# Row-first delta blocks, early output weights, another bank order and a split last merge in a hybrid encoder layer

## The chip, the cores and the metric

The kernel runs on one core of a Trainium2 chip. A core has a matrix engine (TensorE, PE in the profile), three engines for elementwise work (VectorE or DVE, ScalarE or ACT, GpSimd or POOL) and SyncE (SP), which here issues most DMAs. Each engine works through its own list in order and waits on semaphores for others. The metric is device time in microseconds (us), the median of several runs.

## The reference

```python
def reference(x, mix_norm_gain, w_in, ..., w_ff1, w_ff2):     # SEQ = D_MODEL = 1024, D_FF = 4096
    u = rms_norm(h, mix_norm_gain)
    aq, ak, av, dqkv, dgate, da, db = jnp.split(u @ w_in, SPLITS, axis=-1)
    o_att = chunked_rel_attention(aq, ak, av, ...)      # 8 heads of 64, chunk 64 + 8 earlier chunks
    o_att = rms_norm(o_att, att_out_gain)
    dq, dk, dv = jnp.split(causal_short_conv(dqkv, dn_conv_w), 3, axis=-1)
    beta, log_decay = ...                               # from db and da
    o_dn = gated_delta_rule(dq, dk, dv, log_decay, beta)   # 4 heads of 128, triangular solve per chunk
    o_dn = rms_norm(o_dn, dn_out_gain) * jax.nn.silu(dgate)
    h = h + jnp.concatenate([o_att, o_dn], axis=-1) @ w_out
    z = rms_norm(h, ffn_norm_gain) @ w_ff1
    return h + jnp.square(jax.nn.relu(z)) @ w_ff2
```

One layer in float32: one projection for both mixers, band attention and a gated delta rule side by side, an output projection with the residual, and a feed-forward part of two large products.

## The kernel before

**Precision.** Every large float32 operand is split in two float32r parts, a high half (suffix `_h`, a cast on ACT) and a low half (`_l`, a subtraction on DVE or POOL); a product is three matmuls, high-high, high-low, low-high (`mm3`, L222). `split` (L203 and L204) records both halves, so these two lines stand for all operands, and the tile's name tells which.

**Stages.** Projections of delta q, k, v, gate, attention k and q run until about 290 us; `delta_prep` runs beside them. Attention and the chunked delta recurrence are interleaved until about 547, `out_proj` (tiles `op`, 4 groups of 96 matmuls) until 648, `ff1` (`q`, `yy`) until 954, `ff2` (`p`, `y`) to the end. `ff1` and `ff2` are seven-product schemes on 2 x 2 blocks.

**What sets the order.** The code is written as generators. In `attention` a planner (`Clock`, with costs per step) picks which generator goes on: score, turn, flip, a delta step, values, or a step of `outputs_gen`. The framework's scheduler then orders the instructions of each engine by priority (program order, raised inside `tc.high_priority()`) and by its own timeline; `tc.issue_after` holds an instruction behind another. Tiles come from pools with a fixed number of slots: a new tile waits until the last reader of the old one in its slot is done. The pool `wr` has 3 slots and holds raw weights (`wo_4_r` and so on), some attention pages (`t_pb`) and the residual pages `op_x`.

**Delta blocks.** `delta_prep` writes a 128 x 128 matrix per chunk and head to DRAM (`a_dr`), reads its 32 x 32 diagonal blocks back as 128 small systems (`ad`), inverts them by 31 steps on DVE, and writes the inverses (`x_dr`) and their transposes (`y_dr`). `delta_low(b)` (b = 0 in the projection stage, b = 1 in the attention stage) loads inverses and off-diagonal blocks into `l_xa` (L633, L634) and transposes into `l_w` (L630), then multiplies on PE in the 32 x 32 tiles `l_p` (L640, L649). `delta_merge` goes from 64 to 128. Later `c_` tiles are the recurrence: `c_kt`, `c_jv`, `c_jg`, `c_jq` are its loads, `c_att` the masked scores, `c_po` the output, `mixd` the gated result.

**Attention tiles.** `t_sa` and `t_sb` are scores, `t_pa` and `t_pb` probabilities, `t_tpa` and `t_tpb` their transposes on PE ("flips"), copied to `t_ta` and `t_tb`; `t_o` is the product with values, `t_on` its transposed and normalised form, `mixa` the result.

**Output projection.** `mixed` splits `mixd` and `mixa` into `mh` and `ml`; `weights(j)` loads eight 128 x 512 pieces of `w_out` in the order 4, 5, 6, 7, 0, 1, 2, 3 and splits them into `wo_k_h` and `wo_k_l`, the low halves by turns on POOL and DVE (`lo_turn`); `rows` does the matmuls and adds the residual (`h`, L1223).

**Banks.** The eight PSUM banks are dealt to pools in the order in which the pools are made: `ps_a` (3), `ps_t` (2), `ps_o` (1), `ps_d` (2). `op` lies in `ps_a`. After the mixer the same banks are dealt again to `psw` of `ff1` and `ff2`, in tiles of two banks.

**End.** In the last block of `ff2`, `merge` adds one accumulator to another in two halves of 128 x 1024; `store` issues two DMAs of the result. The last product is done by rows, and its four parts are subtracted (L1566) and stored one after the other.

Of the kernel before, what the change touches and what calls it, by code (L numbers as in the profile page):

```python
# [43 lines left out]
NV = 6  # L44
# [54 lines left out]
def hymba_kernel(  # L99
# [31 lines left out]
    mpool = mixer.enter_context(tc.tile_pool(name="mpool", bufs=1))  # L131
    ps_a = mixer.enter_context(tc.tile_pool(name="ps_a", bufs=3, space=PS))
    ps_t = mixer.enter_context(tc.tile_pool(name="ps_t", bufs=2, space=PS))
    ps_o = mixer.enter_context(tc.tile_pool(name="ps_o", bufs=1, space=PS))
    ps_d = mixer.enter_context(tc.tile_pool(name="ps_d", bufs=2, space=PS))

    def page(tag, name, dt=F32, w=512):
# [64 lines left out]
    def split(src, hi, lo, hi_eng, lo_eng):  # L202
        a = nc.scalar.copy(hi, src) if hi_eng is nc.scalar else hi_eng.tensor_copy(hi, src)  # L203
        return a.ins, lo_eng.tensor_tensor(lo, src, hi.bitcast(F32), ALU.subtract).ins  # L204

    lo_turn = [0]

    def load_w(src, name, tags=("wh", "wl")):
        raw = page("wr", name + "_r")
        nc.sync.dma_start(out=raw, in_=src)  # L210
        hi = page(tags[0], name + "_h", F32R)
        lo = page(tags[1], name + "_l", F32R)
        lo_turn[0] += 1
        split(raw, hi, lo, nc.scalar, nc.gpsimd if lo_turn[0] % 2 else nc.vector)
        return hi, lo
# [77 lines left out]
    dg_dr = dram.tile([NT, P, 4, P], F32, name="dg_dr")  # L293
    a_dr = dram.tile([NT, P, 512], F32, name="a_dr")
    x_dr = dram.tile([NT * 4, 32, 4, 32], F32, name="x_dr")
    y_dr = dram.tile([NT * 4, 32, 4, 32], F32, name="y_dr")
    kt_dr = dram.tile([NT, P, 512], F32, name="kt_dr")
# [248 lines left out]
    def delta_prep(kT, ab):  # L546
# [4 lines left out]
        for c in range(NT):  # L551
            n = f"d{c}"
            h4 = slice(4 * c, 4 * c + 4)
            tp = bank(ps_d, n + "_tp")
            four_t(tp, head(kT[c]))
            ss = sumsq(page("pp", n + "_sq"), "p", tp, n)
            if c + 1 < NT:
                kt = page("pp", n + "_kt")
                nc.vector.tensor_tensor(b4(kt), b4(tp), bc_row(ab["edec"][:, 1, h4]), ALU.mult)
                nc.sync.dma_start(out=kt_dr[c], in_=kt)  # L560
            yield 500
            L = decay("pp", n + "_L", ab, h4, tri_s, tri_ur, nc.vector)
            r = rsqrt("p", ss, 4, 1.0, EPS, n)
            br, br2 = ab["br"][:, h4], ab["br2"][:, h4]
            nc.gpsimd.tensor_tensor(br, ab["beta"][:, h4], r, ALU.mult)
            nc.gpsimd.tensor_tensor(br2, br, r, ALU.mult)
            nc.gpsimd.tensor_tensor(ab["nbr"][:, h4], br2, ab["ned"][:, h4], ALU.mult)
            yield 500
            mp = bank(ps_d, n + "_m")
            four(mp, lambda h, hs: kT[c][:, hs], lambda h, hs: kT[c][:, hs])  # L570
            A = page("pp", n + "_A")
            for h in range(4):
                hs = slice(h * P, (h + 1) * P)
                nc.vector.scalar_tensor_tensor(
                    A[:, hs], mp[:, hs], ab["br2"][:, 4 * c + h:4 * c + h + 1], L[:, hs],
                    ALU.mult, ALU.mult)
            nc.sync.dma_start(out=a_dr[c], in_=A)
            yield 900
# [3 lines left out]
        td = page("pp", "td")  # L582
        for c in range(NT):
            for b in range(4):
                bs = slice(32 * b, 32 * b + 32)
                p0 = 16 * c + 4 * b
                nc.sync.dma_start(out=ad[p0:p0 + 4],
                                  in_=a_dr[c].rearrange("r (h e) -> h r e", h=4)[:, bs, bs])
        nc.gpsimd.memset(xf, 0.0)
# [12 lines left out]
        for dst, src in ((x_dr, xd), (y_dr, ad)):  # L602
            for h in range(4):
                nc.sync.dma_start(out=dst[:, :, h, :], in_=src.rearrange("(q h) r e -> h q r e", h=4)[h])

# [11 lines left out]
    def delta_low(b, W, tag):  # L617
# [5 lines left out]
        Y = [w.rearrange("p (c h e) -> p c h e", c=2, h=4) for w in W[-2:]]  # L623
        a4 = a_dr[4 * b:4 * b + 4].rearrange("c r (h e) -> c r h e", h=4)
        for i in range(2):
            nc.gpsimd.memset(W[-2 + i], 0.0)
        for c in range(4):
            q = 16 * b + 4 * c
            for k in range(4):
                nc.sync.dma_start(out=Y[c // 2][32 * k:32 * k + 32, c % 2, :, 32 * (k % 2):32 * (k % 2) + 32],  # L630
                                  in_=y_dr[q + k])
            for r0 in (0, 64):
                nc.sync.dma_start(out=XA[r0:r0 + 32, c], in_=x_dr[q + r0 // 32])  # L633
                nc.sync.dma_start(out=XA[r0 + 32:r0 + 64, c], in_=a4[c, r0 + 32:r0 + 64, :, r0:r0 + 32])  # L634
        yield clock.now + 8000, "d"
# [22 lines left out]
    def delta_merge(c, W, res):  # L658
# [5 lines left out]
        Yd = W[c // 2].rearrange("p (c h e) -> p c h e", c=2, h=4)[:, c % 2]  # L664
        nc.sync.dma_start(out=A[64:128], in_=a_dr[c].rearrange("r (h e) -> r h e", h=4)[64:128, :, 0:64])
        nc.gpsimd.memset(Y[64:128, :, 0:64], 0.0)
# [161 lines left out]

    def attention(after, delta, values, outputs):

# [266 lines left out]
        while True:  # L1097
# [69 lines left out]
            elif k == "score":  # L1167
                g, t, pp = units[begun]
                score(g, t, pp)
                begun += 1  # L1170
                if pp and begun + 2 < len(units):
                    start(*units[begun + 2][0:2])
# [12 lines left out]

    def out_proj(result):


        order = (4, 5, 6, 7, 0, 1, 2, 3)
        w, parts, R, begun = [], [], {}, []  # L1190

        def weights(j):
            w.append([None] * NKT)
            for k in order:
                w[j][k] = load_w(w_out[k * P:(k + 1) * P, j * 512:(j + 1) * 512], f"wo{j}_{k}",
                                 (("wh", "u"), ("u", "wl"))[j])

# [37 lines left out]

        weights(0)
        mixed(0)
        acc = yield from rows(0, 0, None)
        weights(1)
        acc = yield from rows(1, 0, acc)  # L1240
# [174 lines left out]
    def ff2(psw, pools):  # L1415
# [52 lines left out]
        for kb in range(nb):  # L1468
# [70 lines left out]
            accumulate(1, product(f"p1{kb}", lambda i: (a11[i], b11[i])))  # L1539
            accumulate(5, product(f"p5{kb}", prep5))  # L1540
            accumulate(2, product(f"p2{kb}", lambda i: (a12[i], b21[i])))
# [13 lines left out]
            if last:  # L1555
                merge(nc.vector, 7, 6)
                merge(nc.vector, 4, 7)
                merge(nc.gpsimd, 5, 7)
                store(y[5], 1, 1, nc.scalar)
# [44 lines left out]
    ab = ab_proj(u)  # L1604
    W, result = [], {}
    after = []
# [5 lines left out]
    clock.reset()  # L1612
    rest = attention(after[NV - 1], delta_all(ab, kT, W), values, lambda: out_proj(result))
    for _ in rest or ():
# [52 lines left out]
```

## Time and profile before

| | |
|---|---|
| median of 3 runs | 1276.42 us (1275.62 to 1279.3) |
| profiled execution | 1273.11 us, span 1271.0 us |
| granted clock of TensorE, mean | 0.995 |
| PE busy | 1241.2 us, 98% of the span |
| DVE, ACT, POOL busy | 926.5, 547.6, 289.8 us |
| DMA | 158.53 MB, mean 125 GB/s |

The span counts from the first to the last recorded instruction; the execution's own time has 2.1 us around it. A matmul of 128 x 512 is shown with the time from its start to its end, which overlaps the next one's. The clock column is the share of full speed that the chip granted TensorE. "[3.63 <-issue]" behind an instruction says that its engine sat idle for 3.63 us before it and what ended that.

### The profile page before, as it was taken

How to read it: one execution, taken by the hardware profiler on the slowest of the kernel's cores; microseconds unless marked ns; L12 is line 12 of the kernel's file. 1: busy time of each engine (PE TensorE's matmuls, PEld its weight loads, DVE VectorE, ACT ScalarE, POOL GpSimd, SP SyncE). 2: the span in 40 equal slices, each digit the busy share in tenths (PEclk: the TensorE clock that was granted, in tenths of full speed). 3: DMA queues.
4: the chain of work that ended last, by engine and by line, in shares of the span. 5: the costliest groups of instructions: out<-in, count | busy, mean ns of one | idle time of the engine just before them, and what ended most of it. 6: DMA issues, size and time to landing. Idle time of an engine off the chain costs nothing.

```text
span 1271.0 us, 18018 instructions
## 1 busy us (share of the span) xinstructions
PE 1241.2 (98%) x6686; PEld 1033.3 (81%) x6686; DVE 926.5 (73%) x1388; ACT 547.6 (43%) x899; POOL 289.8 (23%) x487
## 2 busy tenths in 40 slices
PE   9999999999998999889999999999999999999998
PEld 8778878778888898778878788888887888888886
DVE  7899987654236577774349777677669997997988
ACT  7323132232245665654445454544445543333331
POOL 4425461344132345543210000000000000000034
PEclk9999999999999999989999999999999999999999
DMA  7214353564585532134441333332259623332002
GB/s 226 67 42 139 101 157 107 121 162 118 175 245 150 162 109 71 40 109 133 141 141 67 116 133 117 132 100 96 86 199 368 211 83 112 121 100 94 7 34 99
DMA packets 135398, 158.53 MB, mean 125 GB/s; under 512 B 31760, under 2 KB 79376, under 8 KB 134800
## 3 DMA queue, kind: packets, MB, share of 16 engines
q1 hardware_dynamic: 117216, 135.11, 35.0%
q10 hardware_dynamic: 18096, 22.29, 5.2%
q8 instruction: 52, 0.85, 0.3%
q14 instruction: 34, 0.28, 0.1%
HBM read 109.91 MB, written 47.45 MB: 124 GB/s over the span
## 4 chain that ended last, share of the span: by engine, by line
PE 51%; DVE 8%; issue 2%; ACT 1%; POOLq 1%; POOL 0%; DVEq 0%; ACTq 0%
PE p L1439 21%; PE q L1343 20%; PE op L222 6%; PE t_o L1024 1%; POOLq L1662 1%; DVE ml L204 1%; DVE h L1285 1%; DVE y L1511 0%; PE t_sa L925 0%; DVE q_0a_l L204 0%; DVE y L1507 0%; PE t_tpb L985 0%; DVE p43b_l L204 0%; DVE p73b_l L204 0%; DVE p43a_l L204 0%
## 5 line engine op out<-in xcount | busy, mean ns | idle before, releaser
L1511 POOL TENSOR_TENSOR y<-y,y 128x1024 f32<-128x1024 f32 x6 | 19.3, 3242 | 590.5 <-DVE y L1507 571.6
L1507 DVE TENSOR_TENSOR y<-y,p 128x1024 f32<-128x1024 f32 x46 | 55.1, 1216 | 5.4 <-PE p L1439 4.5
L222 PE MATMUL op<-mh,wo_l 128*128 128x512 f32 x128 | 50.1, 399 | 1.1 <-POOL wo_l L204 1.1
L222 PE MATMUL op<-mh,wo_h 128*128 128x512 f32 x128 | 50.6, 398 | 0.1
L222 PE MATMUL op<-ml,wo_h 128*128 128x512 f32 x128 | 50.2, 395 | 0.0
L945 DVE CUSTOM_DVE_ANT_0 t_pb<-t_sb,biasn 128x256 f32<-128x256 f32 (+1 forms) x64 | 23.2, 401 | 29.8 <-PE t_sb L925 29.8
L964 ACT ACTIVATE t_pb<-t_pb,t_nm 128x256 f32<-128x256 f32 (+1 forms) x64 | 31.4, 491 | 18.1 <-DVE t_nm L956 16.7
L1223 DVE TENSOR_TENSOR h<-op,op_x 128x512 f32<-128x512 f32 x16 | 10.8, 687 | 28.8 <-PE op L222 28.8
L1230 POOL TENSOR_TENSOR op_q<-op_q 128x512 f32<-128x512 f32 x14 | 19.6, 1397 | 47.3 <-ACT op_q L1229 47.2
L222 PEld LDWEIGHTS op<-mh,wo_l 128*128 128x128 f32 x128 | 24.4, 191 | 6.9 <-POOL wo_l L204 1.5
L222 PEld LDWEIGHTS op<-mh,wo_h 128*128 128x128 f32 x128 | 24.4, 191 | 5.9 <-issue 0.5
L222 PEld LDWEIGHTS op<-ml,wo_h 128*128 128x128 f32 x128 | 24.4, 190 | 5.2
L956 DVE CUSTOM_DVE_ANT_0 t_pa<-t_sa,biaso,t_nm 128x384 f32<-128x384 f32 (+2 forms) x48 | 25.0, 543 | 2.3 <-PE t_sa L925 2.0
L222 PE MATMUL g_ps<-uh,wg_h 128*128 128x512 f32 x64 | 25.3, 396 | 1.2 <-ACT wg_h L203 1.2
L968 ACT ACTIVATE t_pa<-t_pa,t_nm 128x384 f32<-128x384 f32 (+2 forms) x48 | 26.4, 550 | 0.0
L222 PE MATMUL aq_ps<-waq_h,uh 128*128 128x512 f32 x64 | 25.4, 400 | 0.8 <-ACT waq_h L203 0.8
L925 PE MATMUL t_sb<-ks,t_q 128*128 128x256 f32 (+1 forms) x144 | 24.0, 294 | 1.7 <-DVE t_nm L945 1.3
L222 PE MATMUL g_ps<-uh,wg_l 128*128 128x512 f32 x64 | 25.2, 393 | 0.4 <-POOL wg_l L204 0.4
L222 PE MATMUL dq_ps<-uh,wdq_h 128*128 128x512 f32 x64 | 25.5, 398 | 0.0
L222 PE MATMUL dv_ps<-uh,wdv_l 128*128 128x512 f32 x64 | 25.4, 397 | 0.0
L222 PE MATMUL dq_ps<-ul,wdq_h 128*128 128x512 f32 x64 | 25.3, 395 | 0.0
L222 PE MATMUL av_ps<-wav_l,uh 128*128 128x512 f32 x64 | 25.2, 394 | 0.0
(1109 smaller groups left out, 4306.7 us busy)
## 6 DMA issues: line engine op xcount, KB each, us to landing
wa<-in_w_ff_dram SPq DMA_DIRECT2D x32, 512.0 KB
a<-in_w_ff_dram SPq DMA_DIRECT2D x32, 512.0 KB
b<-f_dr SPq DMA_DIRECT2D x32, 512.0 KB
f_dr<-yy ACTq DMA_DIRECT2D x16, 512.0 KB
t_q<-q_dr SPq DMA_DIRECT2D x30, 256.0 KB
f_dr<-zz ACTq DMA_DIRECT2D x13, 512.0 KB
ks<-k_dr SPq DMA_DIRECT2D x16, 256.0 KB
wo_r<-in_w_out_dram SPq DMA_DIRECT2D x16, 256.0 KB
```

The lines of the kernel that those rows point to most:

```text
L204: return a.ins, lo_eng.tensor_tensor(lo, src, hi.bitcast(F32), ALU.subtract).ins
L222: nc.tensor.matmul(ps, a, b, start=(first and i == 0), stop=(last and i == n - 1))
L925: nc.tensor.matmul(o, q[m][:, i * P:(i + 1) * P], k[:, c], start=(m == 0), stop=(m == 1))
L945: nc.vector.tensor_tensor_reduce(sb[:, c], bk[:, c], new[g][pp][:, c], -1.0, 3.0e38, ALU.add, ALU.min, nm[:, 4 + i:5 + i])
L956: nc.vector.tensor_tensor_reduce(sa[e][:, 0:wa], bk[:, 0:wa], old[g][i][:, 384 - wa:384], -1.0, nm[:, 4 + i:5 + i], ALU.add, ALU.min, nm[: ...
L964: nc.scalar.activation(sb[:, c], sb[:, c], AF.Exp, bias=m, scale=-1.0, accum_out=T["sums"][:, 4 + i:5 + i])
L968: nc.scalar.activation(sa[e][:, 0:wa], sa[e][:, 0:wa], AF.Exp, bias=m, scale=-1.0, accum_out=T["sums"][:, i:i + 1])
L1230: nc.gpsimd.tensor_tensor(acc, acc, sq, ALU.add)
L1343: nc.tensor.matmul(part(ps, q), l[:, s], r, start=(k + m == 0), stop=(k == 3 and m == 2))
L1439: nc.tensor.matmul(part(ps[q], 0) if by_rows else part(ps[q // 2], q % 2), l[:, s], part(r, k), start=(i + k + m == 0), stop=(i + k + m == 4))
L1507: nc.vector.tensor_tensor(y[i][m], y[i][m], ps[m], op)
L1511: eng.tensor_tensor(y[i][m], y[i][m], y[z][m], ALU.add)
```

## The change

Six edits. (1) `a_dr`, `x_dr` and `y_dr` lie in DRAM with the row within a block first and the block second, so that several chunks go in one DMA: the loads of `ad` become 16 instead of 32, of each `delta_low` 4 instead of 16 for `l_xa` and 8 instead of 16 for `l_w`; the 128 systems of `ad` are ordered accordingly. (2) The first half of the output weights is emitted inside `attention`, right behind the last score, at high priority, instead of at the start of `out_proj`. (3) All low halves of output weights are made on DVE. (4) The pool `ps_a` is made last of the four bank pools. (5) The second product (`p5`) of `ff2`'s first block is emitted at high priority. (6) The second half of the last addition of `y[7]` to `y[5]` is done on DVE instead of POOL.

```diff
-    ps_a = mixer.enter_context(tc.tile_pool(name="ps_a", bufs=3, space=PS))
     ps_t = mixer.enter_context(tc.tile_pool(name="ps_t", bufs=2, space=PS))
     ps_o = mixer.enter_context(tc.tile_pool(name="ps_o", bufs=1, space=PS))
     ps_d = mixer.enter_context(tc.tile_pool(name="ps_d", bufs=2, space=PS))
+    ps_a = mixer.enter_context(tc.tile_pool(name="ps_a", bufs=3, space=PS))
...
-    def load_w(src, name, tags=("wh", "wl")):
+    def load_w(src, name, tags=("wh", "wl"), low=None):
...
-        split(raw, hi, lo, nc.scalar, nc.gpsimd if lo_turn[0] % 2 else nc.vector)
+        split(raw, hi, lo, nc.scalar, low or (nc.gpsimd if lo_turn[0] % 2 else nc.vector))
...
-    a_dr = dram.tile([NT, P, 512], F32, name="a_dr")
-    x_dr = dram.tile([NT * 4, 32, 4, 32], F32, name="x_dr")
-    y_dr = dram.tile([NT * 4, 32, 4, 32], F32, name="y_dr")
+    a_dr = dram.tile([P, NT, 512], F32, name="a_dr")
+    x_dr = dram.tile([32, NT * 4, 4, 32], F32, name="x_dr")
+    y_dr = dram.tile([32, NT * 4, 4, 32], F32, name="y_dr")
...
-        for c in range(NT):
+        for c in range(0, NT, 2):
             for b in range(4):
                 bs = slice(32 * b, 32 * b + 32)
-                p0 = 16 * c + 4 * b
-                nc.sync.dma_start(out=ad[p0:p0 + 4],
-                                  in_=a_dr[c].rearrange("r (h e) -> h r e", h=4)[:, bs, bs])
+                p0 = 4 * (NT * b + c)
+                nc.sync.dma_start(out=ad[p0:p0 + 8],
+                                  in_=a_dr[:, c:c + 2].rearrange("r c (h e) -> (c h) r e", h=4)[:, bs, bs])
...
-            for h in range(4):
-                nc.sync.dma_start(out=dst[:, :, h, :], in_=src.rearrange("(q h) r e -> h q r e", h=4)[h])
+            for p0 in range(0, P, 32):
+                nc.sync.dma_start(out=dst.rearrange("r q h e -> (q h) r e")[p0:p0 + 32], in_=src[p0:p0 + 32])
...
-        for c in range(4):
-            q = 16 * b + 4 * c
+        for r in range(2):
+            q = 2 * r * NT + 4 * b
+            nc.sync.dma_start(out=XA[64 * r:64 * r + 32], in_=x_dr[:, q:q + 4])
+            nc.sync.dma_start(out=XA[64 * r + 32:64 * r + 64],
+                              in_=a4[64 * r + 32:64 * r + 64, :, :, 64 * r:64 * r + 32])
+        for i in range(2):
             for k in range(4):
-                nc.sync.dma_start(out=Y[c // 2][32 * k:32 * k + 32, c % 2, :, 32 * (k % 2):32 * (k % 2) + 32],
-                                  in_=y_dr[q + k])
-            for r0 in (0, 64):
-                nc.sync.dma_start(out=XA[r0:r0 + 32, c], in_=x_dr[q + r0 // 32])
-                nc.sync.dma_start(out=XA[r0 + 32:r0 + 64, c], in_=a4[c, r0 + 32:r0 + 64, :, r0:r0 + 32])
+                q = k * NT + 4 * b + 2 * i
+                nc.sync.dma_start(out=Y[i][32 * k:32 * k + 32, :, :, 32 * (k % 2):32 * (k % 2) + 32],
+                                  in_=y_dr[:, q:q + 2])
...
                 begun += 1
+                if begun == len(units):
+                    with tc.high_priority():
+                        weights()
...
+    def out_weights(w, j):
+        w.append([None] * NKT)
+        for k in order:
+            w[j][k] = load_w(w_out[k * P:(k + 1) * P, j * 512:(j + 1) * 512], f"wo{j}_{k}",
+                             (("wh", "u"), ("u", "wl"))[j], nc.vector)
...
-        weights(0)
         mixed(0)
         acc = yield from rows(0, 0, None)
-        weights(1)
+        out_weights(w, 1)
...
-            accumulate(5, product(f"p5{kb}", prep5))
+            with tc.high_priority() if not kb else ExitStack():
+                ps = product(f"p5{kb}", prep5)
+            accumulate(5, ps)
...
-                merge(nc.gpsimd, 5, 7)
+                for m, eng in enumerate((nc.gpsimd, nc.vector)):
+                    eng.tensor_tensor(y[5][m], y[5][m], y[7][m], ALU.add)
                 store(y[5], 1, 1, nc.scalar)
...
-    rest = attention(after[NV - 1], delta_all(ab, kT, W), values, lambda: out_proj(result))
+    rest = attention(after[NV - 1], delta_all(ab, kT, W), values,
+                     lambda: out_weights(w_o, 0), lambda: out_proj(result, w_o))
```

**SP at the loads of delta block 1** (`l_xa<-x_dr`: inverses, `l_xa<-a_dr`: off-diagonal blocks, `ks`, `t_q`: attention loads). Before:

```order
L633 DMA l_xa<-x_dr 32x128
L634 DMA l_xa<-a_dr 32x4x32
L858 DMA ks_3991<-k_dr 128x512
L858 DMA ks_3993<-k_dr 128x512
L633 DMA l_xa<-x_dr 32x128
L703 DMA c_kt<-kt_dr 128x512
L634 DMA l_xa<-a_dr 32x4x32
```

Twelve more `l_xa` loads follow, again by turns from `x_dr` and `a_dr`, and then `c_jv`. Now:

```order
L907 DMA t_q<-q_dr 64x2x512 x2
L629 DMA l_xa<-x_dr 32x512
L630 DMA l_xa<-a_dr 32x16x32
L860 DMA ks_3955<-k_dr 128x512
L860 DMA ks_3957<-k_dr 128x512
L629 DMA l_xa<-x_dr 32x512
L705 DMA c_kt<-kt_dr 128x512
L630 DMA l_xa<-a_dr 32x16x32
L702 DMA c_jv<-dv_dr 128x512
```

Four loads are left, each with four chunks, and the last one stands behind `c_kt`, where the fourth stood.

**PE at the end of attention** (`mh`, `ml`: the mixers' result, high and low; `wo_4`: the first piece of the output weights). Before:

```order
L1001 MATMUL t_tpa_6515<-ident,t_pa_6327 128x128 x3
L516 MATMUL c_po<-c_vn,c_att 128x128 x4
L222 MATMUL op_6685<-mh_6650,wo_4_h 128x512
L222 MATMUL op_6742<-mh_6650,wo_4_h 128x512
L222 MATMUL op_6785<-mh_6650,wo_4_h 128x512
L222 MATMUL op_6685<-ml_6651,wo_4_h 128x512
L222 MATMUL op_6742<-ml_6651,wo_4_h 128x512
L222 MATMUL op_6785<-ml_6651,wo_4_h 128x512
L1001 MATMUL t_tpa_6521<-ident,t_pa_6334 128x128 x3
L985 MATMUL t_tpb_6533<-ident,t_pb_6403 128x128 x4
L1001 MATMUL t_tpa_6540<-ident,t_pa_6415 128x128 x3
L1001 MATMUL t_tpa_6546<-ident,t_pa_6422 128x128 x3
```

Now:

```order
L1051 MATMUL t_on<-ident,t_pb_6116 128x128 x2
L1003 MATMUL t_tpa_6507<-ident,t_pa_6271 128x128 x3
L222 MATMUL op_6629<-mh_6594,wo_4_h 128x512
L222 MATMUL op_6686<-mh_6594,wo_4_h 128x512
L222 MATMUL op_6729<-mh_6594,wo_4_h 128x512
L516 MATMUL c_po<-c_vn,c_att 128x128 x4
L222 MATMUL op_6629<-ml_6595,wo_4_h 128x512
L222 MATMUL op_6629<-mh_6594,wo_4_l 128x512
L222 MATMUL op_6629<-mh_6598,wo_5_h 128x512
L222 MATMUL op_6686<-ml_6595,wo_4_h 128x512
L222 MATMUL op_6686<-mh_6594,wo_4_l 128x512
L222 MATMUL op_6686<-mh_6598,wo_5_h 128x512
```

The 36 matmuls of pieces 4 to 7 for three rows of `op` stand ahead of the second `t_tpb` flip; before, only six did.

**DVE at the same place.** Before, from the last read of a row's maximum on:

```order
L956 ISA t_nm 128x1
L807 SCALAR_TENSOR_TENSOR mixd_6009<-c_tpo,dng,c_jg 128x4x128
L780 TENSOR_TENSOR c_att<-c_mt,c_Lt 128x512
L1051 TENSOR_TENSOR t_on<-t_on,t_tot 128x256
L204 TENSOR_TENSOR ml_6651<-mixd_4680,mh_6650 128x512
L786 TENSOR_TENSOR c_o<-c_o,c_po 128x512
L204 TENSOR_TENSOR ml_6655<-mixd_4680,mh_6654 128x512
```

And further down, the first low halves of the output weights that DVE made:

```order
L1036 RECIPROCAL t_tot<-t_tot 128x4
L1006 COPY t_ta_6550<-t_tpa_6546 128x384
L204 TENSOR_TENSOR wo_5_l<-wo_5_r,wo_5_h 128x512
L1068 TENSOR_TENSOR mixa_6257<-t_tpo,again 128x4x128
L204 TENSOR_TENSOR wo_7_l<-wo_7_r,wo_7_h 128x512
```

Now:

```order
L958 ISA t_nm 128x1
L204 TENSOR_TENSOR wo_4_l<-wo_4_r,wo_4_h 128x512
L204 TENSOR_TENSOR wo_5_l<-wo_5_r,wo_5_h 128x512
L204 TENSOR_TENSOR wo_6_l<-wo_6_r,wo_6_h 128x512
L809 SCALAR_TENSOR_TENSOR mixd_5953<-c_tpo,dng,c_jg 128x4x128
L782 TENSOR_TENSOR c_att<-c_mt,c_Lt 128x512
L1053 TENSOR_TENSOR t_on<-t_on,t_tot 128x256
L204 TENSOR_TENSOR ml_6595<-mixd_4624,mh_6594 128x512
L204 TENSOR_TENSOR ml_6599<-mixd_4624,mh_6598 128x512
```

The three low halves stand ahead of `mixd`, `c_att` and `t_on`.

**ACT behind it.** Now:

```order
L203 CAST mh_6602<-mixd_4624 128x512
L1058 ACTIVATE t_on,t_oss<-t_on 128x512
L203 CAST wo_7_h<-wo_7_r 128x512
L203 CAST mh_6606<-mixd_4624 128x512
L203 CAST wo_0_h<-wo_0_r 128x512
L203 CAST wo_1_h<-wo_1_r 128x512
L541 ACTIVATE c_po<-c_o 128x512
L203 CAST wo_2_h<-wo_2_r 128x512
L203 CAST wo_3_h<-wo_3_r 128x512
L1008 COPY t_ta_6511<-t_tpa_6507 128x384
L1008 COPY t_ta_6517<-t_tpa_6513 128x384
```

Before, no cast of a weight stood ahead of these copies: the rows from `t_on` on were

```order
L1056 ACTIVATE t_on,t_oss<-t_on 128x512
L203 CAST mh_6662<-mixd_4680 128x512
L541 ACTIVATE c_po<-c_o 128x512
L1006 COPY t_ta_6525<-t_tpa_6521 128x384
L203 CAST mh_6674<-mixa_5563 128x512
L203 CAST mh_6678<-mixa_5563 128x512
L991 COPY t_tb_6538<-t_tpb_6533 128x512
L1006 COPY t_ta_6544<-t_tpa_6540 128x384
L203 CAST wo_7_h<-wo_7_r 128x512
```

The two `t_ta` copies now stand behind five casts of weights (`wo_7_h` to `wo_3_h`).

Around `p50b_l` the rows of PE, DVE and ACT are the same as before.

More of the change, by code (lines that the diff above doesn't have):

```diff
@@ L576, in delta_prep @@
                     ALU.mult, ALU.mult)
-            nc.sync.dma_start(out=a_dr[c], in_=A)
+            nc.sync.dma_start(out=a_dr[:, c], in_=A)
             yield 900
@@ L623, in delta_low @@
         Y = [w.rearrange("p (c h e) -> p c h e", c=2, h=4) for w in W[-2:]]
-        a4 = a_dr[4 * b:4 * b + 4].rearrange("c r (h e) -> c r h e", h=4)
+        a4 = a_dr[:, 4 * b:4 * b + 4].rearrange("r c (h e) -> r c h e", h=4)
         for i in range(2):
             nc.gpsimd.memset(W[-2 + i], 0.0)
-        for c in range(4):
-            q = 16 * b + 4 * c
-            for k in range(4):
-                nc.sync.dma_start(out=Y[c // 2][32 * k:32 * k + 32, c % 2, :, 32 * (k % 2):32 * (k % 2) + 32],
-                                  in_=y_dr[q + k])
-            for r0 in (0, 64):
-                nc.sync.dma_start(out=XA[r0:r0 + 32, c], in_=x_dr[q + r0 // 32])
-                nc.sync.dma_start(out=XA[r0 + 32:r0 + 64, c], in_=a4[c, r0 + 32:r0 + 64, :, r0:r0 + 32])
+        for r in range(2):
[4 more added lines that the diff above has]
+        for i in range(2):
+            for k in range(4):
+                q = k * NT + 4 * b + 2 * i
+                nc.sync.dma_start(out=Y[i][32 * k:32 * k + 32, :, :, 32 * (k % 2):32 * (k % 2) + 32],
+                                  in_=y_dr[:, q:q + 2])
         yield clock.now + 8000, "d"
@@ L664, in delta_merge @@
         Yd = W[c // 2].rearrange("p (c h e) -> p c h e", c=2, h=4)[:, c % 2]
-        nc.sync.dma_start(out=A[64:128], in_=a_dr[c].rearrange("r (h e) -> r h e", h=4)[64:128, :, 0:64])
+        nc.sync.dma_start(out=A[64:128], in_=a_dr[:, c].rearrange("r (h e) -> r h e", h=4)[64:128, :, 0:64])
         nc.gpsimd.memset(Y[64:128, :, 0:64], 0.0)
@@ L827, in delta_all, with attention @@
             yield gens
-    def attention(after, delta, values, outputs):
+    def attention(after, delta, values, weights, outputs):
         def bias_page(tag, name):
@@ L1184, in attention, with out_proj @@
         return outputs_gen or outputs()
[L1186 to L1196, printed above, removed]
+    order = (4, 5, 6, 7, 0, 1, 2, 3)
+    def out_weights(w, j):
[3 more added lines that the diff above has]
+                             (("wh", "u"), ("u", "wl"))[j], nc.vector)
+    def out_proj(result, w):
+        parts, R, begun = [], {}, []
         def mixed(hf):
@@ L1604, in hymba_kernel @@
     ab = ab_proj(u)
-    W, result = [], {}
+    W, w_o, result = [], [], {}
     after = []
```

## The prediction

> **What bounds the kernel now.** I read the page's busy table first, then the list of what TensorE (PE) waited for, then stretches of time, then single engines.
>
> ```profile
> span 1271.0 us, 18018 instructions
> PE 1241.2 (98%) x6686; PEld 1033.3 (81%) x6686; DVE 926.5 (73%) x1388; ACT 547.6 (43%) x899; POOL 289.8 (23%) x487
> ```
>
> PE is busy for 98% of the span. The change removes no matmul, so all it can win is time in which PE waits or runs at a lowered clock, and the end behind the last matmul.
>
> ```profile
> PE l_p L640 <- issue: 3.6, 1, 3.6
> PE p L1439 <- DVE p50b_l L204: 1.8, 1, 1.8
> PE op L222 <- POOL wo_l L204: 1.1, 1, 1.1
> PE q L1343 <- DVE h L1223: 0.9, 1, 0.9
> PE aq_ps L222 <- ACT waq_h L203: 0.8, 1, 0.8
> 400.00:410.00 10.00, 6.37 (x87) 5.99 (x85) 3.99 (x14) 2.45 (x8) 2.30 (x8) 0.83 0.51 119
> 545.00:560.00 15.00, 11.11 (x60) 8.30 (x60) 10.97 (x20) 9.22 (x21) 8.89 (x16) 0.77 0.37 121
> 960.00:980.00 20.00, 18.21 (x81) 14.76 (x80) 18.53 (x17) 11.83 (x12) 0.00 (x0) 1.00 1.03 391
> ```
>
> The first five are waits (total, times, longest); every part of the change points at one of them. The last three are stretches: length, busy time of PE, of its weight loads, DVE, ACT, POOL, then granted clock. At 400 PE was idle 3.63 us and the clock was 0.83, which costs another 0.17 x 10 = 1.7. At 545 it was idle 3.89, and the clock of 0.77 cost 0.23 x 15 = 3.45. At 960 a wait of 1.79 left the clock at 1.00. So two places hold 5.3 and 7.3 us, and the others nothing but their waits.
>
> **Delta block 1, loads in fewer pieces.**
>
> ```profile
> DMA  4978699999999999999995121011021021021165
> 390.87 0.58 SPq L633 DMA_DIRECT2D l_xa<-x_dr  x1
> 403.56 0.55 SPq L634 DMA_DIRECT2D l_xa<-a_dr  x1
> 399.86 1.06 PE L516 MATMUL c_pq<-state,c_jq 128*128 128x128 f32 x8
> 404.55 1.44 PE L640 MATMUL l_p<-l_w,l_xa 32*32 32x32 f32 x32 [3.63 <-issue]
> ```
>
> These two SP rows are the first and last of 16 l_xa loads on SP's queue, one about every 0.6 us; PE begins l_p 0.44 us behind the last one's issue (404.11). So the wait that the profile calls "issue" is SP working through the list. Now four loads do it, each four times as large. The fifth to sixteenth (12 x 0.6 = 7 us or more) go, and the last stands where the third and fourth now stand, near 395.5; beside the transfers queued there it should land by 399, before 400.92, where PE is done with c_pq. PE's own order here is the same before and after. The wait and the clock loss go together: between 3.6 (clock dips anyway) and 5.3. I take 5.0, nearer the upper end, because the low clock starts right behind this wait. Late next would be t_q or c_jv, which move up on SP with it. New on SP: wo_4_r to wo_6_r stand earlier, between the l_w loads, and may wait there for a buffer that PE's t_on still reads. Behind them wait t_q and l_xa, but 16 fewer l_w issues (some 9 us) stand against it. I cost that at 0.
>
> The DMA line (the 40 slices of 388 to 406) shows the 16 DMA engines full until about 398 and nearly idle from there to 404. [...]
>
> **Delta block 0, in the projection stage.**
>
> ```profile
> 247.75 5.07 SPq L630 DMA_DIRECT2D l_w<-y_dr  x8
> 261.96 1.19 PE L640 MATMUL l_p<-l_w,l_xa 32*32 32x32 f32 x32
> 271.11 0.73 PE L222 MATMUL aq_ps<-waq_h,uh 128*128 128x512 f32 x2 [0.84 <-ACT waq_h L203]
> ```
>
> Here 8 x_dr loads become 2 and 16 l_w loads 8: 6 x 0.58 + 8 x 0.63 = 8.5 us less on SP, so the data that allowed l_p at 261.96 is there by 253.4. But the new order also puts l_p 39 rows earlier on PE, 39 x 0.23 (the pace of such rows, below) = 9 us, at 253.0. PE arrives as the data does: a wait of 0 to 1.5 (the 0.4 between them, and two loads more). Behind these loads the waq_r loads move up too, and the 0.84 wait for waq_h should go. Net between -0.84 and +1.5; I take -0.3, nearer to the wait that a row shows.
>
> **Output weights early, low halves on DVE.**
>
> ```profile
> 646.30 0.39 PE L222 MATMUL op<-mh,wo_h 128*128 128x512 f32 x1
> ...
> 647.45 0.39 PE L222 MATMUL op<-mh,wo_l 128*128 128x512 f32 x1
> 560.00:648.00 88.00, 87.70 (x411) 71.46 (x407) 33.62 (x41) 34.08 (x55) 27.54 (x26) 1.00 0.37 122
> 545.35 0.49 PE L1001 MATMUL t_tpa<-ident,t_pa 128*128 128x128 f32 x3
> 549.74 0.66 PE L985 MATMUL t_tpb<-ident,t_pb 128*128 128x128 f32 x4 [0.78 <-ACT t_on L1056]
> 555.56 0.80 PE L222 MATMUL op<-mh,wo_l 128*128 128x512 f32 x1 [1.14 <-POOL wo_l L204]
> 558.29 0.63 PE L222 MATMUL op<-mh,wo_l 128*128 128x512 f32 x1
> 553.92 3.28 POOL L204 TENSOR_TENSOR wo_l<-wo_r,wo_h 128x512 fp32r<-128x512 f32 x2
> 544.44 0.75 DVE L807 SCALAR_TENSOR_TENSOR mixd<-c_tpo,dng,c_jg 128x512 f32<-128x512 f32 x1
> 545.34 0.69 DVE L780 TENSOR_TENSOR c_att<-c_mt,c_Lt 128x512 f32<-128x512 f32 x1
> 555.54 6.13 SPq L210 DMA_DIRECT2D wo_r<-in_w_out_dram  x5
> 546.00 1.13 ACT L203 CAST mh<-mixd 128x512 fp32r<-128x512 f32 x2
> 558.12 0.62 ACT L203 CAST wo_h<-wo_r 128x512 fp32r<-128x512 f32 x1 [5.14 <-DMA wo_r<-in_w_out_dram]
> ```
>
> The first two rows give the undisturbed pace, five op matmuls in 1.15 us, 0.23 each. Before, PE had only flips (t_tpa, t_tpb) to do around 548 to 555, each waiting for a copy, because no low half of the output weights existed before POOL's 553.92. Now wo_4_l, wo_5_l, wo_6_l are DVE's next rows after the last score, at 544.44, and 36 op matmuls (8 us) stand ahead of those flips. Cost: three subtractions of some 0.65 (c_att's kind of row) push mixd and c_att back by 1.9, so c_att ends at 547.8 instead of 546.0. PE is free at 545.84, waits for the first mh (546.0 + 0.6) 0.75, runs three op matmuls to 547.3, waits 0.4 for c_att, and should then run on: 1.2 of idle left of 7.3, hence 6.1 as the upper end. POOL loses its wo_l rows, and what stood behind them (the gate chain for c_o) comes 3.28 earlier, off PE's path. The next weights' loads start when wo_4_l frees its buffer, near 545.1 instead of 555.54.
>
> The lower end comes from ACT, which works in order: wo_2_h and wo_3_h now stand ahead of two t_ta copies, and PE needs a bank that these free at about 547.3 + 0.4 + 33 x 0.23 + 1.0 (t_tpa, and four c_po at half of c_pq's 1.06) = 556.3. From free buffer (555.54) to cast (558.12) took 2.6 us. By that, wo_3_r lands about 554.5 and the copies are done by 556; slack a few tenths. One load later and PE stops 2.6 us, with a share of the low clock: gain 2. I take 5.0, nearer the upper end, since most of the 7.3 is cover that now exists.
>
> [...]
>
> The later weights (second column half) now load DVE alone with 0.69 each instead of POOL for half of them. From 560 to 648 PE is busy 87.7 us and DVE 33.6 of 88: 0.
>
> **Bank order.**
>
> ```profile
> 647.87 0.69 DVE L1223 TENSOR_TENSOR h<-op,op_x 128x512 f32<-128x512 f32 x1 [4.80 <-PE op L222]
> ```
>
> PE's first q matmul waited 0.9 for this row, which reads a bank that ff1's first tile reuses. With ps_a made last, that tile lies on ps_t's banks, long free: -0.9, or 0 if the add's result itself is needed first. I take -0.9: the operands were ready.
>
> **Product 5 of block 0.** PE, DVE and ACT have the same rows around it as before; "high priority" finds nothing to move. The 1.8 stays. Cost 0, or -1.8 if the start of other work shifts it.
>
> **The last merge.**
>
> ```profile
> 1262.56 1.87 DVE L1566 TENSOR_TENSOR y<-y,p 128x512 f32<-128x512 f32 x3
> 1265.88 0.69 DVE L1566 TENSOR_TENSOR y<-y,p 128x512 f32<-128x512 f32 x1 [1.44 <-PE p L1439]
> 1259.38 7.84 POOL L1511 TENSOR_TENSOR y<-y,y 128x1024 f32<-128x1024 f32 x2 [13.70 <-DVE y L1511]
> 1263.27 3.66 SPq L1567 DMA_DIRECT2D out_dram<-y  x4
> 1264.93 2.70 ACTq L1464 DMA_DIRECT2D out_dram<-y  x2
> ```
>
> POOL's second add ends at 1267.22 and its store is issued to 1267.63, behind SP's last (1266.93); the span ends 3.4 later. DVE takes that add over, twice one of the three half-wide rows (0.62), some 1.2, inside the 1.44 that it idles. The end then hangs on SP's last store, half as large. At least 1267.63 - 1266.93 = 0.7 is won; at most 2.3, if its smaller size also shortens the 3.4. I take 1.7.
>
> **Sum.** -5.0 - 0.3 - 5.0 - 0.9 - 0 - 1.7 = -12.9 against the profiled execution of 1273.1 (span 1271.0 and 2.1 around it): 1260.2. That execution is 3.3 below the median of 1276.4, so against the median 1263.5.
>
> **Rivals.**
> - *ACT's order eats the middle part.* Weight casts wait for loads ahead of t_ta copies: the gain there is 2, the time 1266.5. For it: the 5.14 that ACT once waited for such a load; against it: loads start 10 us earlier.
> [...]
> - *Block 1 keeps its wait*, because transfer of small pieces, not issue, sets it: 1268.5.
> - *Product 5 does move*: 1261.7.
> - *Two of these losses together*, or a new wait in block 0 as well: about 1273, no change that can be told.
> - *Slower*, with these rows:
>
> ```profile
> 371.09 5.40 SPq L630 DMA_DIRECT2D l_w<-y_dr  x6
> 379.56 0.38 PE L1049 MATMUL t_on<-ident,t_pb 128*128 128x128 f32 x2
> 386.60 0.60 SPq L210 DMA_DIRECT2D wo_r<-in_w_out_dram  x1
> ```
>
> SP, strictly in order, stops at wo_4_r for its buffer. The first such load went out at 386.6 before, and now stands behind the first l_w, near 371.7. If the buffer really frees only then, 15 us are lost ahead of l_xa, which goes to 410.5: PE waits 9.7 plus some 2 of clock instead of gaining 5, and the sum is +4: 1280. The sum passes zero where the stop nears 11 us. Against it: t_on, which reads those buffers, is done by 380.
>
> **Chances.** Forecast 0.57 (own range 1260.5 to 1266); ACT's order 0.15; clock 0.06; transfer 0.05; product 5 0.05; two losses 0.08; slower 0.04. A change of 0.3% (3.8 us) is about what a measurement of this kernel can tell: faster than 1272.6 is all but the last two, 0.88; same 0.08; slower 0.04. The range 1258 to 1270 reaches from all the best ends together (-0.8 - 5.3 - 6.1 - 0.9 - 1.8 - 2.3 = -17.2, so 1259.2) and a little more to the three single losses, and leaves out the last two cases.
>
> **What would show it.** Clock 1.00 and no l_p wait in 400:410; in 545:560 PE busy near 14 of 15 at clock 1.00, no wait for wo_l, some 1.2 for mh and c_att; first q matmul without a wait for h; p50b_l's 1.8 unchanged; POOL with one add at the end, and the end about 2 us nearer to the last matmul. I am wrong if a t_tpb or t_tpa waits 2 us or more near 556, if l_p waits near 253 or 396, or if the clock falls without such waits.

## The result, and the profile after

The changed kernel takes 1263.53 us (median of 5, 1262.15 to 1266.24) against 1276.42; the ratio is 0.9901, 95% interval 0.9877 to 0.9925. The forecast was 1263.5. The profiled execution has a span of 1260.4 against 1271.0 and a time of 1262.15: 10.7 shorter in its span, where the prediction's sum was 12.9. So the profile moved less than the medians did, and two terms of the sum were wrong. First the page's top lines, then the list of PE's waits (total, times, longest), then three stretches (length, busy time of PE, PEld, DVE, ACT, POOL, granted clock, DMA share, GB/s) of the kernel after:

```profile
span 1260.4 us, 17948 instructions
PE 1237.4 (98%) x6686; PEld 1030.8 (82%) x6686; DVE 929.2 (74%) x1397; ACT 547.4 (43%) x899; POOL 278.3 (22%) x478
```

```profile
PE p L1444 <- DVE p50b_l L204: 1.8, 1, 1.8
PE ak_tp L485 <- DVE ak_n L480: 1.6, 1, 1.6
PE op L222 <- ACT mh L203: 0.8, 1, 0.8
PE t_sb L927 <- DMA t_q<-q_dr: 0.6, 1, 0.6
```

```profile
400.00:410.00 10.00, 10.00 (x167) 9.21 (x166) 7.16 (x24) 5.61 (x17) 2.74 (x9) 1.00 0.21 63
545.00:560.00 15.00, 15.00 (x77) 12.24 (x76) 10.81 (x20) 7.62 (x15) 5.47 (x14) 1.00 0.36 106
960.00:980.00 20.00, 19.75 (x87) 16.35 (x88) 18.56 (x18) 9.39 (x11) 0.00 (x0) 1.00 0.82 314
```

The l_p wait, the flips' waits, the wait for wo_l, the first q matmul's wait for `h` and the wait for waq_h are gone, and both low clocks with them. What stays is the 1.8 for p50b_l; of the new waits, 0.8 stands before the first op matmul.

To see where the 10.7 came from, I read five points of PE's timeline in the profiled executions listed here: the start of the last `aq_ps` matmul, the first `op`, the first `q`, the first `p`, and the end of the last matmul. The columns are the time to the first point, the stretches between the points, and the rest of the span.

| execution | to last aq | to op | op to q | q to p | p to last | end | span |
|---|---|---|---|---|---|---|---|
| before | 317.8 | 229.2 | 101.7 | 305.3 | 311.9 | 5.2 | 1271.0 |
| before, again | 317.7 | 230.6 | 101.5 | 305.3 | 311.9 | 5.2 | 1272.1 |
| after | 317.9 | 224.2 | 94.7 | 305.2 | 311.9 | 6.5 | 1260.4 |
| after, again | 318.4 | 224.1 | 95.1 | 305.2 | 313.5 | 6.5 | 1262.7 |
| blocks only | 318.5 | 228.2 | 101.7 | 305.3 | 311.9 | 5.2 | 1270.9 |
| weights only | 318.6 | 227.2 | 96.9 | 305.3 | 311.9 | 5.3 | 1265.2 |
| low halves by turns | 318.2 | 226.9 | 94.5 | 305.2 | 313.5 | 6.5 | 1264.8 |
| 32 pieces, row-first | 317.8 | 224.1 | 95.1 | 305.2 | 311.9 | 6.5 | 1260.6 |
| last merge on POOL | 318.5 | 225.5 | 95.3 | 305.2 | 313.5 | 5.2 | 1263.2 |
| last merge on DVE | 318.4 | 226.1 | 95.1 | 305.2 | 311.9 | 5.6 | 1262.3 |

After against before: 0.1 more, 5.0 less, 7.0 less, 0.1 less, nothing, 1.3 more. The gain lies in the attention stage and at its seam with the output projection; the end lost. (The first op matmul now stands ahead of c_po; up to the last c_pq the attention stage is 4.6 shorter, so 0.4 of the 5.0 belongs to the seam.) The sixth column takes only two values in these rows, 311.9 and 313.5; the experiments say why.

At the seam the replay of the prediction came out nearly row for row. PE's and ACT's timelines of after:

```profile
542.11 0.96 PE L222 MATMUL op<-mh,wo_h 128*128 128x512 f32 x3 [0.81 <-ACT mh L203]
551.94 0.60 PE L987 MATMUL t_tpb<-ident,t_pb 128*128 128x128 f32 x4
549.58 0.62 ACT L203 CAST wo_h<-wo_r 128x512 fp32r<-128x512 f32 x1 [1.32 <-DMA wo_r<-in_w_out_dram]
550.80 0.62 ACT L203 CAST wo_h<-wo_r 128x512 fp32r<-128x512 f32 x1 [0.60 <-DMA wo_r<-in_w_out_dram]
551.33 0.85 ACT L1008 COPY t_ta<-t_tpa 128x384 f32<-128x384 f32 x2
```

PE waited 0.81 (predicted 0.75) for the first mh. ACT did wait for the two late weights ahead of the `t_ta` copies, 1.32 and 0.60, and the copies began 0.6 before PE came to the t_tpb that follows: the slack of "a few tenths" held.

At the end, POOL's two additions (min/median/max in ns) and DVE's four before; then, of after, DVE's new addition, POOL's one, DVE's last subtraction and the store queues (SP's small parts, ACT's two large ones):

```profile
L1511 POOL TENSOR_TENSOR y<-y,y x2: 2348/3935/5522, 1259.4 to 1264.9; 128x1024 f32<-128x1024 f32 x2
1258.02 4.62 DVE L1511 TENSOR_TENSOR y<-y,y 128x1024 f32<-128x1024 f32 x4
```

```profile
1250.59 1.21 DVE L1566 TENSOR_TENSOR y<-y,y 128x1024 f32<-128x1024 f32 x1
1247.41 6.66 POOL L1566 TENSOR_TENSOR y<-y,y 128x1024 f32<-128x1024 f32 x1 [13.70 <-DVE y L1516]
1253.91 0.69 DVE L1574 TENSOR_TENSOR y<-y,p 128x512 f32<-128x512 f32 x1 [0.31 <-PE p L1444]
1252.43 2.52 SPq L1575 DMA_DIRECT2D out_dram<-y  x4
1254.10 0.94 ACTq L1469 DMA_DIRECT2D out_dram<-y  x2
```

Before, POOL's two additions took 5.52 and 2.35; the first, now the only one, takes 6.66. It ends 2.3 behind DVE's last addition of y in both kernels (1264.90 behind 1262.64, 1254.07 behind 1251.80), so DVE's new addition, which stands ahead of its three subtractions, puts off POOL's end too. Both large stores therefore start together after 1254, behind the first small ones, instead of one at 1264.93 with 0.9 of matmuls still to run.

### The profile page after: what moved, and what is told of

Its sections match the earlier page's. It is cut to its first block, busy times and chain, and to the rows that moved or that the text cites. A ratio compares the mean times of both kernels' runs of the same rounds, so it can differ in the third digit from the quotient of the medians.

```text
span 1260.4 us, 17948 instructions
## 1 busy us (share of the span) xinstructions
PE 1237.4 (98%) x6686; PEld 1030.8 (82%) x6686; DVE 929.2 (74%) x1397; ACT 547.4 (43%) x899; POOL 278.3 (22%) x478
## 4 chain that ended last, share of the span: by engine, by line
PE 55%; DVE 5%; ACT 1%; issue 1%; POOL 0%; DVEq 0%
PE p L1444 23%; PE q L1348 20%; PE op L222 7%; PE t_o L1026 1%; DVE h L1290 1%; PE t_sa L927 0%; DVE q_0a_l L204 0%; PE t_tpb L987 0%; PE t_tpa L1003 0%; PE t_sb L927 0%; ACT t_pb L966 0%; PE c_pv L516 0%; PE c_po L516 0%; PE t_tpo L520 0%; PE c_pq L516 0%
## 5 line engine op out<-in xcount | busy, mean ns | idle before, releaser
L1516 POOL TENSOR_TENSOR y<-y,y 128x1024 f32<-128x1024 f32 x4 | 11.5, 2896 | 575.6 <-DVE y L1512 570.8
L222 PE MATMUL aq_ps<-waq_l,uh 128*128 128x512 f32 x64 | 25.3, 395 | 0.0
```

The costliest lines, as they stand in the source:

```text
L222: nc.tensor.matmul(ps, a, b, start=(first and i == 0), stop=(last and i == n - 1))
```

## The experiments

**Blocks only** (the row-first arrays and nothing else, on before).

> Before with the row-first blocks alone (edit 1). If the loads of l_xa are bound by SP's issue, the l_p wait of 3.6 and the low clock at 400 go, and TensorE leaves the attention stage some 4.9 earlier; the gaps from 545 to 560 and their low clock stay (7.3). Time about 5 below before: 1271. If the transfers of small pieces set the wait, it stays and the time is before's. [...]

Measured 1271.29 (10 runs) against 1276.59: ratio 0.9957, 0.9937 to 0.9977. The profiled execution took longer than that median, and shows what I had not expected: the l_p wait is gone and another stands in its place. Its waits, and two stretches of PE (busy, clock, DMA share, GB/s):

```profile
PE t_sb L927 <- DMA t_q<-q_dr: 2.0, 1, 2.0
375.00:380.00 5.00, 3.04 (x18) 0.82 0.99 214
380.00:385.00 5.00, 5.00 (x48) 0.84 0.68 200
```

The low clock of 0.82 followed this 1.96 wait as it had followed the l_p wait. On SP the loads of block 1 can't have held up this t_q: SP issued its two loads at 369.4 and 370.7, ahead of the first l_w (374.0), and the second landed 7.2 later, while the DMA engines were full (share 0.99). What made them late is open. Attention is only 1.0 shorter here than before; a second low clock, from 518.14 to 521.55 behind waits that all kernels have, costs another 1.7 of it. The seam is as it was (101.7).

**Weights only** (early emission and all low halves on DVE, on before).

> Before with the early output weights and all low halves on DVE (edits 2 and 3). If the gaps from 545 to 560 come from late low halves, one wait of about 0.8 for mh is left there, the clock stays at 1.00 and some 6 is won: 1270. The l_p wait of 3.6 stays. If ACT's casts hold up the t_ta copies, a t_tpb waits 2 or more and the gain is 2 to 3. If the low clock has a cause other than the gaps, it stays and the gain is about 2.7.

Measured 1266.47 (6 runs): ratio 0.9909, 0.9878 to 0.9941, by the medians far more than the 6 expected; the span of its profile is 5.8 below before's. Op to q fell from 101.7 to 96.9. The l_p wait vanished here too, though nothing was done to its loads:

```profile
PE t_sb L925 <- DMA t_q<-q_dr: 2.5, 2, 2.2
390.00:395.00 5.00, 3.75 (x21) 0.77 0.69 185
```

PE had already lost the time at t_q, earlier on the same queue (2.21, and a clock of 0.77 behind it), and came to the c_pq ahead of l_p 4.4 us later than in before (404.24 against 399.86; 0.8 of it from the start). The t_q loads of this wait went out at 384.6 and 385.8, behind 12 of the 16 l_w loads of block 1. So this t_q wait and l_p's look like two places where one lateness of SP's queue can surface. Which of them shows, and how much, differs by kernel and by execution; that is one reason why medians and single profiles can disagree here.

**The kernel before, again.**

> The kernel before, unchanged, profiled a second time. If the l_p wait of 3.6 with its low clock is a fixed part of the schedule, it is there again within 0.5. If it comes from how transfers fall in one execution, it differs by 1 or more, or another load (t_q) is waited for in its place; the span then differs with it.

The l_p wait was 2.3 this time, t_q's 1.6, and the clock fell behind them:

```profile
PE l_p L640 <- issue: 2.3, 1, 2.3
PE t_sb L925 <- DMA t_q<-q_dr: 1.6, 2, 1.4
400.00:410.00 10.00, 7.68 (x102) 0.82 0.48 119
```

The second branch of the expectation: the two waits share their sum between them (3.6 + 0.4 before, 2.3 + 1.6 now) and are no fixed part of the schedule.

**32 pieces** (after, with the row-first arrays, but loaded in single pieces again).

```diff
-        for r in range(2):
-            ... in_=x_dr[:, q:q + 4] ...
-        for i in range(2):
-            ... in_=y_dr[:, q:q + 2] ...
+        for c in range(4):
+            for k in range(4):
+                ... in_=y_dr[:, k * NT + 4 * b + c]
+            for r in range(2):
+                ... in_=x_dr[:, 2 * r * NT + 4 * b + c] ...
```

> After with the same row-first arrays, but delta_low's loads in 32 single pieces again. If the count of issues on SP sets the wait, l_p waits again for about 3 to 4 and the clock falls at 400; span 1264 to 1266. If the layout in DRAM is what helped, there is no wait and the span is that of after.

No l_p wait, span 1260.6: the count of issues does not set the wait. Time of one issue on SP, min/median/max in ns, before and then in this kernel:

```profile
L630 SPq DMA_DIRECT2D l_w<-y_dr x32: 538/597/811, 247.8 to 385.3; - x32
L634 SPq DMA_DIRECT2D l_xa<-a_dr x16: 544/582/630, 196.3 to 403.6; - x16
```

```profile
L629 SPq DMA_DIRECT2D l_w<-y_dr x32: 302/430/1425, 246.4 to 386.6; - x32
L633 SPq DMA_DIRECT2D l_xa<-a_dr x16: 420/422/455, 196.5 to 399.6; - x16
```

The same number of loads with the same number of bytes takes SP 0.43 instead of 0.60 each (0.42 instead of 0.58). Over the 32 loads of block 1 that is some 5 us, and the last l_xa was issued by 400.0 instead of 404.1, before PE was done with c_pq. In "weights only", with block-first arrays, the medians are 597 and 582 again. So the price of an issue went with the address pattern of the DRAM side here (0.60 and 0.58 us block-first, 0.43 and 0.42 row-first), and either way of saving, the cheaper piece or fewer pieces, is enough. Why the pattern does it is left open; no run took the patterns apart. The 128 B pieces of a_dr are all still here, and the wait is gone: their size alone is not its cause.

**Low halves by turns** (after, without `nc.vector` in `out_weights`).

> After, but the low halves of the output weights made by turns on POOL and DVE as before (edit 3 undone). If early emission alone does it, the span is that of after (1260). If the low halves have to be on DVE, the first one on POOL (1.3 to 1.6 each, in line behind the gate chain) is late: TensorE waits 1 to 2 for wo_l in the first op matmuls, and the span is 1 to 3 longer.

Span 1264.8. It loses 2.8 against after before the first p, but 1.4 of that lies ahead of the last c_pq, where no low half of these weights is made yet; 1.6 more goes in ff2 by a low clock that has nothing to do with it. So 1.5 is left for the edit, in one profile. The place was another than I thought: not PE's wait for wo_l, but DVE's, beside POOL. PE, DVE and POOL of this kernel:

```profile
544.21 1.16 PE L516 MATMUL c_po<-c_vn,c_att 128*128 128x128 f32 x8 [1.54 <-DVE c_att L782]
541.17 1.73 DVE L204 TENSOR_TENSOR wo_l<-wo_r,wo_h 128x512 fp32r<-128x512 f32 x1
539.83 2.52 POOL L204 TENSOR_TENSOR wo_l<-wo_r,wo_h 128x512 fp32r<-128x512 f32 x2
```

While POOL makes two low halves, DVE's takes 1.73, where in after three in a row take 1.89 together. Three on DVE thus take it hardly longer than one beside POOL, and c_att, which PE waits for (1.54), stands behind it.

**The last merge**: both halves on POOL as before, both on DVE, and two ways of storing DVE's half first.

```diff
-                for m, eng in enumerate((nc.gpsimd, nc.vector)):
+                for m, eng, queue in ((1, nc.vector, nc.sync), (0, nc.gpsimd, nc.scalar)):
                     eng.tensor_tensor(y[5][m], y[5][m], y[7][m], ALU.add)
+                    queue.dma_start(out=..., in_=two(y[5][m]))
-                store(y[5], 1, 1, nc.scalar)
```

> After with both halves of the last y[5] addition on POOL again (edit 6 undone). By the prediction's step the end moves 0.7 to 2.3 later behind the last matmul: 7.2 to 8.8 instead of after's 6.5. By the rival, that the split makes the remaining POOL addition slower and sends both large stores together with the last small ones, the end is 5.2 behind the last matmul as in the kernel before, and the split costs 1.3.

> After with both halves of that addition on DVE, none on POOL. DVE's last subtraction moves about 0.8 later (one addition of 1.15 less the 0.31 that it idled), but both large stores go out by about 1253 instead of 1254 and 1255, and no POOL addition of 6.7 is waited for. If the large stores set the end, it is 1 to 2 earlier than after's 6.5 behind the last matmul; if DVE's last store does, it is 0.8 later.

> After with the DVE half added and stored first on ACT's queue, the POOL half second. If the end is set by two 512 KB stores that start together behind POOL's addition, sending one 2 us earlier brings the end 1 to 2 nearer to the last matmul than 6.5. If only the second one counts, nothing changes.

> After with DVE's half of the last addition stored at once on SP's queue, and POOL's half on ACT's. The last 2 MB leave at some 380 GB/s without a pause, so the end should follow the moment when the first of them is issued and DVE's last small store. If so, half a megabyte that starts 0.7 earlier than after's first store brings the end from 6.5 to 5.0 to 5.8 behind the last matmul. If POOL's late half alone sets the end, it stays at 6.5.

From the last matmul to the end: 5.19 with both on POOL, 5.57 with both on DVE, 6.48 with both stores on ACT's queue whatever the order in the code, 5.81 with DVE's half on SP's queue. The third is inconclusive: ACT issued both stores only 0.2 behind the last matmul, when POOL was done, so nothing went out earlier. The fourth moved as expected (5.0 to 5.8), but not past the old form. The split of the changed kernel is the slowest of the four. What the end waits for is seen in DMA's 40 slices, of before from 1256 to 1271, of after from 1245 to 1260.4, and of the kernel with both on DVE from 1252 to 1262.3:

```profile
DMA  9999993000000000000003999999999999993000
```

```profile
DMA  9996000000000000000004999999999999990000
```

```profile
DMA  0000000002999991004999999999999999500000
```

In the first two, the DMA engines are full from the first store to the end, at some 380 GB/s for the 2 MB that are left. The end therefore follows the moment at which these stores begin, not the last one's: they begin 2.6, 2.0 and 1.4 before the end of the last matmul in before, with DVE's half on SP's queue and in after, and the span ends 5.2, 5.8 and 6.5 behind it. That holds only where no pause follows. With both halves on DVE the first large store went out 3.2 before the end of the last matmul, earlier than in any other form, but the next one followed only 2.3 later, the engines stood idle for some 0.6 in between, and the end was 5.6. DVE's extra addition moved the first small store from 2.6 us before the end of the last matmul to 1.4 before it.

**Product 5**, whose edit moved nothing. In the profiles of before and after, every engine has the same rows in the same order from the first p to the end, but for the last addition of edit 6. To test what the wait hangs on, I held three of DVE's additions behind the first p50b_l:

```diff
             def prep3(i):
-                tt(s1[i], s1[i], a11[i], ALU.subtract)
+                with behind():                # tc.issue_after(<first p50b_l>) in block 0
+                    tt(s1[i], s1[i], a11[i], ALU.subtract)
...
             def prep7(i):
-                tt(a21[i], a11[i], a21[i], ALU.subtract)
+                with behind():
+                    tt(a21[i], a11[i], a21[i], ALU.subtract)
```

> After with two edits: three of DVE's additions that stand ahead of the first p50b_l (for products 3 and 7) are held behind it, and the last y[5] addition is back on POOL alone. If DVE's order is what product 5 of block 0 waits for, p50b_l is ready 3.4 earlier, the wait of 1.8 goes, and ff2 takes 310.1 instead of 311.9 (or the 313.5 of the executions in which the clock dipped there). If another input is as late, the wait stays under another name. The end stands 5.2 behind the last matmul.

The wait of 1.8 went, and one of 3.9 came at product 2. PE and ACT of this kernel, and PE's clock from 964 to 974:

```profile
968.34 1.22 PE L1449 MATMUL p<-p20b_h,p20a_h 128*128 128x512 f32 x2 [3.94 <-ACT p20b_h L203]
964.00 0.37 ACTq L1357 DMA_DIRECT2D f_dr<-yy  x1
964.47 1.01 ACT L1515 COPY y<-p 128x1024 f32<-128x1024 f32 x1 [7.56 <-DMA y<-h_dr]
964.00:974.00 10.00, 6.06 (x15) 0.66 1.03 403
```

The edit had let the scheduler put the store of `yy` three rows earlier on ACT. That store went out at 964.0 here and at 963.55 in after. In both it first waited for a semaphore that it shares with one of the loads y<-h_dr on SP, which landed at 963.93 (963.47 in after), 10 us behind its issue, while the DMA engines were full (403 GB/s); only now the copies and casts for product 2 stood behind the store. From the first p to the end of the last matmul it took 316.7, and the end stands 5.4 behind that.

**One addition held, the old last merge** (the version that the experiments point to; ACT's order is that of after up to the casts for product 3), beside the changed kernel on the same chip.

> After with the last addition back on POOL alone and only one of product 3's additions (s1 minus a11) held behind the first p50b_l, which leaves ACT's order as in after. By DVE's order the wait of 1.8 shrinks by one addition, 1.13, to 0.7, and no low clock follows it; ff2 takes 310.8 instead of 311.9 or 313.5. The end stands 5.2 instead of 6.5 behind the last matmul. Together 2.4 to 4 below after: 1260 to 1261. If ACT falls behind a store again as in the run before it, a new wait takes the 1.13 back and more.

> The changed kernel once more, on the same chip as the version with the old tail and the moved addition. 1263.5 as before, between 1262 and 1266.5, spread by how often the clock falls behind the wait of 1.8 in ff2 (1.6 more) and by how long t_q is waited for in the attention stage (0.6 to 2.3).

1262.04 (6 runs, 1261.16 to 1263.38), ratio 0.9907, 0.9884 to 0.9929; the changed kernel 1264.40 (6 runs, 1262.76 to 1266.16), 0.9922, 0.9899 to 0.9946. It is the fastest kernel here, 2.4 below by the medians, though the two ratios' intervals overlap. Its waits in ff2, and the stretch behind the wait of 1.8 in the second profile of after:

```profile
PE p L1449 <- DVE p50b_l L204: 0.6, 1, 0.6
PE p L1449 <- ACT p20b_h L203: 0.4, 1, 0.4
```

```profile
958.00:968.00 10.00, 8.22 (x30) 0.83 1.04 403
```

The wait fell from 1.8 to 0.6 and 0.4 came behind it, so ff2 took 311.4 instead of 311.9, less than the 1.1 expected. In this one profile no clock of 0.83 follows either; that cost 1.6 in the second profile of after, and in three others. The end stands at 5.3.

## Why the prediction was right, and where it was not

- *Block 1* (taken 5.0). Wait and low clock went; to the last c_pq, counted from the last aq, the attention stage is 4.6 shorter. The size held in after, but not in blocks only, where the profile shows 1.0 and the medians 5.3. The step held in half: "fewer issues" is one way, but cheaper issues alone did the same. And the term is not a property of these loads alone: a wait for t_q appears where the one for l_p does not, in blocks only, in weights only, and with 0.6 in after. The prediction named t_q as late next, but meant the loads behind l_xa; those that were waited for stand ahead of it on SP. Its "16 fewer l_w issues (some 9 us)" are 8 fewer in this block (16 became 8), some 5 us; the term stays 0.
- *Block 0* (taken -0.3): the last aq matmul is at 317.9 instead of 317.8. The waq_h wait went, and l_p started at 253.45 without a wait, but ak_tp's wait grew from 1.0 to 1.6.
- *Early weights* (taken 5.0 of 7.3): 0.81 of idle is left and the clock stayed at 1.00, so 6.5 was won, past the upper end of 6.1. The choice below the upper end allowed for a stop at ACT that did not come.
- *Bank order* (taken 0.9): the wait for `h` is there, with 0.9, in all three kernels with the old order (before, blocks only, weights only) and in none with the new one.
- *Product 5* (taken 0): right, for the reason given.
- *The last merge* (taken -1.7, measured +1.3): the failed step. It priced the end by the last store's issue plus a fixed rest of 3.4, and "half as large" as a gain. In fact the end goes by bytes from the first store's issue, and that came 1.1 later: the step put DVE's new addition inside the 1.44 that DVE idles, but it stands ahead of the three subtractions whose parts are stored first. The step also took POOL's first addition to stay as it was in the pair, while it went from 5.52 to 6.66.
- *The median*. In the profile the terms give 10.7, not 12.9, so it is luck that 1263.5 was met to the digit. The profiled execution of before lay 3.3 below its median and that of after only 1.4 below its own, which makes up the difference. The prediction did not count this spread: the 15 runs of before beside the first experiments ran from 1270.5 to 1283.6, and those of after from 1262.2 to 1266.2. Beside the last experiments the medians were 1272.48 (10 runs of before) and 1264.40 (6 of after), only 8.1 apart. The waits on SP's queue, with the low clocks that follow some of them, differ from one profile to the next, which fits a narrower spread where they are short; no run tied a long execution to them.

The rivals: a clock that dips without the gaps did not occur (in after the clock's record is low only from 1256.32 on, behind the last matmul), nor did the stop at wo_4_r. The rival on transfers is refuted for l_p by after and by the 32 pieces, whose 128 B pieces are those of before.

## What to carry to other kernels

A wait at the end of a list of loads is paid by the list: before shortening one entry, ask which earlier load on the queue will be waited for instead, and look at the price of an issue (0.60 or 0.43 us here) as well as at the count. Where stores fill the DMA engines to the end, as they did here at some 380 GB/s, start the first one earlier and leave no pause behind it; moving work so that the last one is ready sooner can cost (6.5 us behind the last matmul here, instead of 5.2). Holding one instruction back can move others on another engine, as it did here for a wait of 3.9: compare every engine's order, and look there for a store that waits ahead of something needed.

## What the runs showed of the hardware

Short gaps were followed by a low clock here, and the same gap not always. A wait of 1.96 (blocks only) had a clock of 0.82 behind it, one of 2.21 (weights only) 0.77. Behind the wait of 1.8 for p50b_l the clock stayed at 1.00 in eight profiled executions and fell in four (low halves by turns, last merge on POOL, the ordered stores, after again), 1.6 us each time. In the clock's own record every low stretch ahead of the kernel's end runs at half clock for 3.41 or 6.83 us (405.20 to 408.61 and 551.97 to 558.80 in before, 962.34 to 965.75 in after again), and within one execution the edges lie a multiple of 3.41 apart (405.20 to 551.97 is 43 times 3.413). Counted from these edges in steps of 3.41, the wait of 1.8 lay inside one step, at least 0.29 from both its edges, in the four executions in which the clock fell (959.22 to 961.00 in after again, in the step from 958.92). In the eight others it crossed an edge or came within 0.12 of one (958.46 to 960.25 in after, with an edge at 959.36). That the outcome depends on where a gap falls between such edges is an estimate from these twelve executions; no run moved the gap alone.

Where POOL and DVE worked side by side, one of them took longer here. In "low halves by turns" a DVE subtraction, of which three take 1.89 in after, took 1.73: it began at 541.17 beside POOL's and ended 0.55 behind them (542.90 and 542.35). At the end of the kernel it is POOL that took longer. Its addition takes 2.35 where DVE idles or subtracts a product, and 5.52 or 6.66 where it starts beside DVE's additions, which take 1.21 with and without it, and it ends 2.3 behind the last of these, which is about its own time. Why is left open.
